# Constant products on TensorE at the heads of stages, and two pieces of VectorE work queued behind others

## The chip, the cores and the metric

The kernel runs on one core of a Trainium2 chip. The metric is the device time of one execution in microseconds; of several executions the median counts. All activations and weights are float32 in HBM.

## The reference, cut to what matters

Two models follow one another on a sequence of 256 positions with 1024 channels. The first has four layers, each an FFN, a mixer and another FFN; the mixers are sliding-window attention (layers 0 and 3), gated linear attention (1) and the recurrent mixer rwkv7 (2). The second has two layers, each a mixer (latent attention, then neighbourhood attention) and a gated FFN with a short convolution.

```python
for layer in range(4):
    ff = swiglu(rmsnorm(h, g[0]), ffn_w_in[layer, 0], ffn_w_out[layer, 0]); h = h + 0.5 * rmsnorm(ff, g[1])
    u = rmsnorm(h, g[2]);  m = (swa_attention, gla_attention, rwkv7_time_mix)[layer % 3](u, ...)
    h = h + rmsnorm(m, g[3])
    ff = swiglu(rmsnorm(h, g[4]), ffn_w_in[layer, 1], ffn_w_out[layer, 1]); h = h + 0.5 * rmsnorm(ff, g[5])
...
def step(state, inp):                 # rwkv7, one position; 16 heads of 64
    r_t, w_t, k_t, v_t, a_t, b_t = inp
    sa = jnp.einsum('bhij,bhj->bhi', state, a_t)
    state = state * w_t[:, :, None, :] + sa[..., None] * b_t[:, :, None, :] + v_t[..., None] * k_t[:, :, None, :]
    return state, jnp.einsum('bhij,bhj->bhi', state, r_t)
...
h_lat = layer_norm(DEEPNORM_ALPHA * h_lat + g1 * y, ln1_g[i], ln1_b[i])          # y from mla_mixer / na_mixer
h_lat = layer_norm(DEEPNORM_ALPHA * h_lat + g2 * conv_ffn(modulate(h_lat, sh2, sc2), ...), ln2_g[i], ln2_b[i])
```

## The kernel before

The 256 positions are two tiles of 128 partitions (`t`). Every large product is made of three fp32r products (`mm3`, L116 to L118): each operand is split into a rounded part (`whi`, `xTh`, by a copy on ScalarE, L81) and the rest (`wlo`, `xTl`, by a subtraction on VectorE, L82). `wchunk` loads a weight chunk of 128x1024 into one of four staging buffers (`st`) and splits it; `wblock` and `wmat` call it. With `held` at 0 the two split instructions are queued behind the two instructions in `split` on their engines (`issue_after`), with `held` above 0 that many chunks go before that. PSUM has three rings: `psG` (tag `G`, 2 buffers) for projections and scores, `psT` (tag `pt`, 2) for transposes and `psO` (tag `po`, 4) for accumulators. A scheduler puts the instructions of each engine in a fixed order before the run, by program order and by when it expects each to be ready; an engine then works its own list strictly in that order. `issue_after` adds an edge for the order of one engine only.

- `ffn1_body`: eleven blocks `j`, both tiles in each; first products into `G` from the transposed input `xT`.
- `swa_body`: after the projections, for each tile and for blocks of four or two heads (512 columns) scores `S`, masked softmax, transposes `pT`, product with `v`.
- `gla_body`: `proj(b)` yields a product `G` for each tile; block 1 (keys) is the first.
- `rwkv_body`: channels in two halves `q`. At its start the normalised input is transposed (`un`, `pt`, L771 to L774), then come projections, and `part1(0)`, `part2(0)`, `part1(1)`, `merges(0)`, `part2(1)`, `part3(0)`, `merges(1)`, `part3(1)`. `part1(q)` makes decays, normalised keys and the matrices `ar`, `bk`, `L` for each tile and stores `L` to DRAM. `part2(q)` reads the 16x16 diagonal blocks back (`comp`), inverts them in 15 steps of a product and a reduction on VectorE (L950, L951), copies the transpose (L952), stores both and reloads the full matrices `T` and `Z`. `merges(q)` builds the inverse of the 128x128 blocks from them (L964). `part3(q)` runs the chain R (`psR`, L1030), U (`psU`, L1036), Y (`psY`, L1055, L1057), the state, and the output norm; the gate product `psg` (L1096, L1097) stands at its end.
- `Block2.mod_T`: transposes `h` and scales it; called at the head of both mixers (`mod_tile`) and after each output tile (`conv_in`).
- `Block2.na` and `na_attn`: for each tile and each of 16 heads a score product `S` (L1598), a bias on VectorE (L1600), `softmax`, and `pv` (transposes `pP`, L1301; copy `PT`, L1303; products with `v`). The splits of `w_o` for the output product come after it in the program.

## Time and profile before

| | |
|---|---|
| median of 3 executions | 3358.42 us (3358.12 to 3369.33) |
| profiled execution, its own time | 3367.27 us |
| its span | 3365.5 us, 45238 instructions |
| TensorE products busy | 3190.7 us (95%), 16491 |
| VectorE, ScalarE, GpSimd busy | 2340.0 us (70%), 1596.2 us (47%), 161.6 us (5%) |
| mean granted clock of TensorE | 0.969 |
| HBM traffic | 156 GB/s over the span |

The profile is of one execution. Busy time of TensorE includes the time in which a product is under way, so it is not TensorE at its peak. PE is TensorE, PEld its weight loads, DVE is VectorE, ACT is ScalarE, POOL is GpSimd, SP the queue of most DMAs. The granted clock is 1.00 at 2.4 GHz and 0.50 at 1.2 GHz. L12 is line 12 of the kernel. An idle time stands in square brackets, with what ended it.

### The profile page before, as it was taken

What the parts mean: (1) busy time and instruction counts of PE and PEld (TensorE: products, weight loads), DVE (VectorE), ACT (ScalarE), POOL (GpSimd) and SP (SyncE); (2) the same over time, 40 slices, a digit from 0 to 9 for tenths busy, and PEclk for the clock granted to TensorE, in tenths of its full rate; (3) what the DMA queues carried; (4) which work ended last, traced back from release to release, by engine and by line L of the source; (5) the groups of instructions that cost most, each with busy time, mean ns of one, the idle gap of its engine ahead of it and who ended that gap; (6) DMA issues with size and microseconds to landing.
All of it is one profiled execution on the core that took longest, in us unless ns stands there. A gap on an engine that the chain in (4) does not pass through costs nothing. (4 is left out here: it accounts for less than half of the span.)

```text
span 3365.5 us, 45238 instructions
## 1 busy us (share of the span) xinstructions
PE 3190.7 (95%) x16491; PEld 2620.0 (78%) x16491; DVE 2340.0 (70%) x3767; ACT 1596.2 (47%) x2734; POOL 161.6 (5%) x248
## 2 busy tenths in 40 slices
PE   8999999989999988899999999999999999998898
PEld 7877877877887766687878877887777887775797
DVE  6767767677767766656776676765579877637787
ACT  5455454455445465224454464545544434424453
POOL 0001000000000001001010001010000000011000
PEclk9999999999999999779999999999999999998899
DMA  7653657643766753414656645631027554431463
GB/s 241 214 200 97 219 181 227 217 138 107 231 207 194 231 166 92 117 41 138 219 181 221 198 135 188 219 116 52 15 69 226 170 161 138 143 105 42 150 183 100
DMA packets 424667, 529.12 MB, mean 157 GB/s; under 512 B 54982, under 2 KB 342792, under 8 KB 424444
## 3 DMA queue, kind: packets, MB, share of 16 engines
q1 hardware_dynamic: 416124, 523.86, 49.7%
q10 hardware_dynamic: 8320, 2.36, 0.3%
q8 instruction: 130, 2.13, 0.3%
q14 instruction: 93, 0.76, 0.1%
HBM read 520.35 MB, written 5.78 MB: 156 GB/s over the span
## 5 line engine op out<-in xcount | busy, mean ns | idle before, releaser
L82 DVE TENSOR_TENSOR wlo<-st,whi 128x1024 fp32r<-128x1024 f32 (+1 forms) x810 | 974.8, 1216 | 406.4 <-ACT whi L81 371.6
L81 ACT CAST whi<-st 128x1024 fp32r<-128x1024 f32 (+1 forms) x810 | 835.5, 1044 | 532.3 <-PE po L118 171.3
L118 PE MATMUL G<-whi,xTl 128*128 128x512 f32 x1792 | 708.5, 396 | 19.8 <-DVE xTl L183 19.1
L116 PE MATMUL G<-whi,xTh 128*128 128x512 f32 x1792 | 714.1, 399 | 8.5 <-ACT xTh L802 1.9
L117 PE MATMUL G<-wlo,xTh 128*128 128x512 f32 x1792 | 705.3, 394 | 3.8 <-DVE wlo L79 3.8
L118 PEld LDWEIGHTS G<-whi,xTl 128*128 128x128 f32 x1792 | 338.5, 189 | 97.4 <-DVE xTl L183 27.1
L116 PEld LDWEIGHTS G<-whi,xTh 128*128 128x128 f32 x1792 | 338.8, 189 | 78.4 <-ACT xTh L802 3.1
L117 PEld LDWEIGHTS G<-wlo,xTh 128*128 128x128 f32 x1792 | 339.0, 189 | 71.9 <-DVE wlo L79 5.7
L116 PE MATMUL po<-whi,hh 128*128 128x512 f32 x968 | 379.6, 392 | 9.1 <-ACT hh L260 7.2
L117 PE MATMUL po<-wlo,hh 128*128 128x512 f32 x968 | 377.6, 390 | 0.0
L118 PE MATMUL po<-whi,hl 128*128 128x512 f32 x968 | 339.9, 392 | 1.0 <-DVE hl L1750 0.5
L1714 PE MATMUL G<-xh,whi 128*128 128x256 f32 (+1 forms) x720 | 244.2, 340 | 9.1 <-ACT ub L1718 5.7
L1715 PE MATMUL G<-xl,whi 128*128 128x256 f32 (+1 forms) x720 | 242.2, 336 | 0.8 <-DVE xl L1239 0.8
L1716 PE MATMUL G<-xh,wlo 128*128 128x256 f32 (+1 forms) x720 | 241.7, 336 | 0.0
L251 ACT ACTIVATE sg<-G,rpre 128x256 f32<-128x256 f32 x176 | 83.8, 476 | 290.3 <-PE G L118 285.9
L116 PEld LDWEIGHTS po<-whi,hh 128*128 128x128 f32 x968 | 181.8, 188 | 50.6 <-ACT hh L260 10.9
L118 PEld LDWEIGHTS po<-whi,hl 128*128 128x128 f32 x968 | 180.5, 188 | 40.2 <-DVE hl L261 2.0
L117 PEld LDWEIGHTS po<-wlo,hh 128*128 128x128 f32 x968 | 181.8, 188 | 37.1
L1182 DVE SCALAR_TENSOR_TENSOR aa<-aw,sc,aa 128x1024 f32<-128x1024 f32 x140 | 174.9, 1282 | 46.8 <-DMA aw<-in_ada_w_dram 46.3
L1714 PEld LDWEIGHTS G<-xh,whi 128*128 128x128 f32 x720 | 139.1, 193 | 23.6 <-ACT ub L1718 6.1
L1715 PEld LDWEIGHTS G<-xl,whi 128*128 128x128 f32 x720 | 139.2, 193 | 15.2 <-DVE xl L1239 1.3
L1716 PEld LDWEIGHTS G<-xh,wlo 128*128 128x128 f32 x720 | 138.9, 193 | 14.3
(483 smaller groups left out, 4350.1 us busy)
## 6 DMA issues: line engine op xcount, KB each, us to landing
st<-in_ffn_w_in_dram SPq DMA_DIRECT2D x704, 256.0 KB, 4.2
st<-in_ffn_w_out_dram SPq DMA_DIRECT2D x242, 512.0 KB, 4.1
aw<-in_ada_w_dram SPq DMA_DIRECT2D x96, 512.0 KB, 4.5
st<-in_ffn_w_in_dram SPq DMA_DIRECT2D x88, 512.0 KB, 5.0
st<-in_swa_w_qkv_dram SPq DMA_DIRECT2D x24, 512.0 KB, 4.8
st<-in_gla_w_in_dram SPq DMA_DIRECT2D x24, 512.0 KB, 4.5
st<-in_rwkv_w_rkv_dram SPq DMA_DIRECT2D x24, 512.0 KB, 4.6
st<-in_na_w_qkv_dram SPq DMA_DIRECT2D x24, 512.0 KB, 4.2
```

What stands on the lines that cost most here:

```text
L81: nc.scalar.copy(hi, st)
L82: nc.vector.tensor_sub(lo, st, hi)
L116: m(out, xh, wh, start=start, stop=False)
L117: m(out, xh, wl, start=False, stop=False)
L118: return m(out, xl, wh, start=False, stop=stop)
L251: nc.scalar.activation(sg, G[:, :256], AF.Tanh, scale=rs[t][1])
L1182: nc.vector.scalar_tensor_tensor(acc[s], st, x, acc[s], op0=OP.mult, op1=OP.add)
L1714: m(Gf[:, a:b], wh, xh[:, k, a:b], start=(k == 0 and a == 0), stop=False, **kw)
L1715: m(Gf[:, a:b], wh, xl[:, k, a:b], start=False, stop=False, **kw)
L1716: m(Gf[:, a:b], wl, xh[:, k, a:b], start=False, stop=(k == 7 and b == ns * 256), **kw)
```

## The change

A tile of ones, 128x1 in bf16, is made once, and a method `warm(ps, n)` issues `n` products of it (both operands by broadcast, so 128x128 against 128 x columns) into the PSUM tile that the next real product overwrites with `start=True`. It is called in ten functions. `psg` in `part3` moves up ahead of Y. In `part1(1)` everything of the second tile is traced under `issue_after(zc[0])`, so its VectorE instructions are queued behind the last copy of `part2(0)`. In `na` the splits of `w_o` are queued behind the copy `PT` and the bias of the fourth head of the first tile. The pad of the small pool shrinks by 32 bytes. Lines that only gain an indentation are left out here.

```diff
+        self.one_ = self.consts.tile([128, 1], BF16, name="one_")
+        nc.vector.memset(self.one_, 1.0)
+    def warm(self, ps, n):
+        o = ps if len(ps.shape) == 2 else ps.rearrange("p a b -> p (a b)")
+        k = o.shape[1]
+        for _ in range(n):
+            self.nc.tensor.matmul(o, self.one_.to_broadcast([128, o.shape[0]]), self.one_.to_broadcast([128, k]),
+                                  start=True, stop=True, skip_group_check=True)
...
# ffn1_body
                 G = self.psG.tile([128, 512], F32, name="G", tag="G")
+                if (j, t) == (0, 0):
+                    self.warm(G, 3)
# swa_body
             S = c.psG.tile([128, nh, nk], F32, name="S", tag="G")
+            if (nb == 1 and h0) or (t and h0 < 8):
+                c.warm(S, 3)
# gla_body, proj
+            if b == 1 and t == 0:
+                c.warm(G, 8)
# rwkv_body, front, for each t and q
             pt = c.psT.tile([128, 4, 128], F32, name="pt", tag="pt")
+            c.warm(pt, 6)
# part1
         for t in TT:
+            with c.tc.issue_after(zc[0].ins) if q and t else nullcontext():
...
                     pb = c.psT.tile([128, 2, 129], F32, name="pb", tag="pt")
+                    if q and a == 0:
+                        c.warm(pb, 5)
...
                     pt = c.psT.tile([128, 4, 128], F32, name="pt", tag="pt")
+                    if q:
+                        c.warm(pt, 2)
...
                     ps = c.psO.tile([128, 4, 128], F32, name="psL", tag="po")
+                    if q:
+                        c.warm(ps, 2)
# part2
-        nc.vector.tensor_copy(Zc, Tc.rearrange("p a b -> p b a"))
+        zc[q] = nc.vector.tensor_copy(Zc, Tc.rearrange("p a b -> p b a"))
# merges
-        def four(a, lhs, rhs, pool, tag):
+        def four(a, lhs, rhs, pool, tag, n=0):
             ps = pool.tile([128, 4, 128], F32, name="ps4", tag=tag)
+            c.warm(ps, n)
...
-                    ps = four(a, lambda hh: L[t, q][:, hh], lambda hh: Z[t, q][:, hh], c.psO, "po")
+                    ps = four(a, lambda hh: L[t, q][:, hh], lambda hh: Z[t, q][:, hh], c.psO, "po",
+                              16 if (q, t, a, B) == (0, 0, 0, LEV[0]) else 0)
# part3
             pu = c.psO.tile([128, 8, 64], F32, name="psU", tag="po")
+            c.warm(pu, 2)
...
             nc.scalar.copy(U, pu)
+            pg = c.psG.tile([128, 512], F32, name="psg", tag="G")
+            c.warm(pg, 2)
...
                 nc.tensor.matmul(py[:, hh], MB[hh % 2][:, hh // 2], hv(U)[:, hh], start=False, stop=(hh == 7),
                                  skip_group_check=True)
+                if hh % 2 and hh < 7:
+                    c.warm(pg, 1)
+            nc.tensor.matmul(pg, gmT[:, 0, t * 128:t * 128 + 128], g2a, start=True, stop=False)
+            nc.tensor.matmul(pg, gmT[:32, 1, t * 128:t * 128 + 128], g2b[:32], start=False, stop=True)
...
-            pg = c.psG.tile([128, 512], F32, name="psg", tag="G")
-            nc.tensor.matmul(pg, gmT[:, 0, t * 128:t * 128 + 128], g2a, start=True, stop=False)
-            nc.tensor.matmul(pg, gmT[:32, 1, t * 128:t * 128 + 128], g2b[:32], start=False, stop=True)
# Block2.mod_T
             pt = c.psT.tile([128, 4, 128], F32, name="pt", tag="pt")
+            if t < 2:
+                c.warm(pt, 4)
# Block2.pv(..., warm=0)
         pt = c.psT.tile([128, 4, 128], F32, name="pP", tag="pt")
+        c.warm(pt, warm)
...
-        nc.scalar.copy(PT, pt)
+        self.turned = nc.scalar.copy(PT, pt)
# Block2.na
+            c.split, c.held = self.begun, 0
             wo = c.wblock(w_o, 0, 8, 0, D)
+            c.held = -1
# Block2.na_attn
                     S = c.psG.tile([128, 512], F32, name="S", tag="G")
+                    if t == 0 and hh < 4:
+                        c.warm(S, 3)
...
-                            [[v[x][:, hh // 2, 64 * (hh % 2):64 * (hh % 2) + 64] for x in (2, 3, 0, 1)]], rev)
+                            [[v[x][:, hh // 2, 64 * (hh % 2):64 * (hh % 2) + 64] for x in (2, 3, 0, 1)]], rev,
+                            4 if t == 0 and hh < 3 else 0)
+                    if (t, hh) == (0, 3):
+                        self.begun = self.turned, biased
```

## Rows read from the trace of the kernel before

**Rows 1.** Span, first to last instruction, and mean granted TensorE clock.
```profile
core 0: 3365.5 us, clock 0.969
```
**Rows 2.** Stretches: length; busy PE, PEld, DVE, ACT, POOL; PEclk, DMA share, GB/s.
```profile
246.00:282.00 36.00, 31.20 (x232) 24.59 (x231) 31.00 (x92) 24.69 (x92) 0.00 (x0) 0.91 0.17 56
...
1340.00:1386.00 46.00, 30.55 (x116) 21.92 (x116) 31.42 (x77) 6.39 (x15) 3.81 (x4) 0.51 0.35 89
...
1426.00:1462.00 36.00, 34.32 (x157) 28.61 (x157) 14.56 (x31) 7.50 (x12) 1.93 (x2) 0.51 0.20 54
1503.00:1525.00 22.00, 20.21 (x168) 16.69 (x167) 13.69 (x31) 3.85 (x8) 1.90 (x2) 1.00 0.08 25
...
3018.00:3044.00 26.00, 16.70 (x64) 8.69 (x64) 18.75 (x35) 11.05 (x21) 2.75 (x1) 0.74 0.36 113
...
3139.00:3172.00 33.00, 20.49 (x122) 18.46 (x121) 28.69 (x51) 15.91 (x26) 2.82 (x4) 0.74 0.60 190
```
**Rows 3.** Timeline of TensorE, single products: start, length, engine, line, operation [idle before].
```profile
698.97 0.63 PE L116 MATMUL G<-whi,xTh 128*128 128x512 f32 x1
699.39 0.63 PE L117 MATMUL G<-wlo,xTh 128*128 128x512 f32 x1
...
1007.87 0.19 PE L1203 MATMUL psa<-one,ab 128*128 128x1 bf16 x2
...
1329.96 0.39 PE L118 MATMUL G<-whi,xTl 128*128 128x512 f32 x1
1330.18 0.39 PE L116 MATMUL G<-whi,xTh 128*128 128x512 f32 x1
...
1499.55 1.08 PE L1096 MATMUL psg<-g2a,gmT 128*128 128x512 f32 x2
```
**Rows 4.** Waits of TensorE: total us, times, longest us.
```profile
PE G L118 <- DVE xTl L183: 19.1, 14, 3.4
...
PE pt L773 <- ACT un L771: 9.9, 2, 7.3
```
**Rows 5.** Timeline of VectorE, first and last of eleven operations, and the copy.
```profile
1363.19 0.42 DVE L875 TENSOR_SCALAR th<-th 128x512 f32<-128x512 f32 x1
...
1371.96 0.68 DVE L926 TENSOR_TENSOR bk<-pt,E 128x512 f32<-128x512 f32 x1
...
1373.55 0.38 DVE L952 COPY Zc<-Tc 128x256 f32<-128x256 f32 x1
```
**Rows 6.** Timeline of TensorE, first merge products of each half.
```profile
1386.45 6.43 PE L964 MATMUL ps<-Z,L 128*128 128x128 f32 x30 [12.24 <-DMA Z<-Zd]
...
1471.52 1.95 PE L964 MATMUL ps<-Z,L 128*128 128x128 f32 x16
```
**Rows 7.** Timeline of TensorE, the four psU of part3.
```profile
1426.91 3.67 PE L1036 MATMUL psU<-W,Z 128*128 128x64 f32 x16 [1.27 <-ACT W L1033]
...
1457.62 3.68 PE L1036 MATMUL psU<-W,Z 128*128 128x64 f32 x16
...
1503.47 2.00 PE L1036 MATMUL psU<-W,Z 128*128 128x64 f32 x16
...
1522.18 2.00 PE L1036 MATMUL psU<-W,Z 128*128 128x64 f32 x16
```
**Rows 8.** Timeline of TensorE, transposes in mod_T.
```profile
2252.11 1.03 PE L1229 MATMUL pt<-ident,h 128*128 128x128 f32 x8
```
**Rows 9.** Timeline of VectorE, ScalarE and TensorE at the neighbourhood attention.
```profile
3026.56 1.23 DVE L82 TENSOR_TENSOR wlo<-st,whi 128x1024 fp32r<-128x1024 f32 x1
...
3028.20 1.04 ACT L81 CAST whi<-st 128x1024 fp32r<-128x1024 f32 x1 [1.68 <-DMA st<-in_na_w_o_dram]
...
3029.97 2.07 PE L1598 MATMUL S<-kT,qT 64*128 64x512 f32 x2 [8.25 <-ACT P L1284]
...
3044.11 1.46 PE L1598 MATMUL S<-kT,qT 64*128 64x512 f32 x4
...
3048.39 1.45 PE L1598 MATMUL S<-kT,qT 64*128 64x512 f32 x4
```

More of the change, by code (lines that the diff above doesn't have):

```diff
@@ L1 @@
 import math
-from contextlib import ExitStack
+from contextlib import ExitStack, nullcontext
 import numpy as np
@@ L886, in part1 @@
-            Es[t] = E1, E2
-            e = mix.tile([128, 4], F32, name=f"em{t}{q}")
-            nc.vector.tensor_copy(e, E2[:, :, 0] if t else E1[:, :, 128])
-            E1m[t, q] = e
-            z = c.psO.tile([128, 512], F32, name="z", tag="po")
-            nc.tensor.matmul(z, waT[1][:, t * 128:t * 128 + 128], wa2[1][:65], start=True, stop=True)
-            th_a[t] = tmp("tha")
-            nc.scalar.activation(th_a[t], z, AF.Tanh, scale=0.5)
-            km = tmp("km", 1)
-            nc.vector.scalar_tensor_tensor(km, th_a[t], -1.0, kab, op0=OP.add, op1=OP.mult)
@@ L907, in part1 @@
-            b2 = th_a[t]
-            nc.vector.scalar_tensor_tensor(b2, b2, 1.0, kn, op0=OP.add, op1=OP.mult)
-            bo = tmp("bo")
-            nc.vector.tensor_mul(bo, r[t, q], km)
-            nc.vector.tensor_mul(bo, bo, rkb)
-            bon[t, q] = mix.tile([128, 8], F32, name=f"bon{t}{q}")
-            nc.vector.tensor_reduce(bon[t, q], hv(bo), axis=AX.X, op=OP.add)
-            if not q:
-                ar[t, q], bk[t, q] = ring([128, 4, 2, 128], "ar"), ring([128, 4, 2, 128], "bk")
-            else:
-                ar[t, q] = c.act.tile([128, 4, 2, 128], F32, name="ar", tag="xTh")
-                bk[t, q] = c.act.tile([128, 4, 2, 128], F32, name="bk", tag="xTl")
@@ L920, in part1 @@
-            E1, E2 = Es[t]
-            for x, dst, e in ((kn, ar[t, q][:, :, 0], E1[:, :, :128]), (r[t, q], ar[t, q][:, :, 1], E1[:, :, 1:]),
-                              (b2, bk[t, q][:, :, 0], E2[:, :, 1:]), (km, bk[t, q][:, :, 1], E2[:, :, 1:])):
-                pt = c.psT.tile([128, 4, 128], F32, name="pt", tag="pt")
-                for ch in range(4):
-                    nc.tensor.transpose(pt[:, ch], x[:, ch * 128:(ch + 1) * 128], c.ident)
-                nc.vector.tensor_mul(dst, pt, e)
@@ L927, in part1 @@
-            L[t, q] = ring([128, 8, 128], "L")
-            for a in range(2):
-                ps = c.psO.tile([128, 4, 128], F32, name="psL", tag="po")
-                for i in range(4):
-                    p = slice(64 * a, 64 * a + 64)
-                    nc.tensor.matmul(ps[:, i], ar[t, q][p, i, 0], bk[t, q][p, i, 0], start=(i == 0),
-                                     stop=(i == 3), skip_group_check=True)
-                nc.vector.tensor_mul(L[t, q][:, 4 * a:4 * a + 4], ps, mL.unsqueeze(1).to_broadcast([128, 4, 128]))
@@ L939, in part2 @@
+    T, Z, zc = {}, {}, {}
     def part2(q):
@@ L1294, in more, with pv @@
         return self.c.work.tile(shape, F32, name=name, tag=tag)
-    def pv(self, M, out, P, vs, order=None):
+    def pv(self, M, out, P, vs, order=None, warm=0):
         c, nc = self.c, self.c.nc
         pt = c.psT.tile([128, 4, 128], F32, name="pP", tag="pt")
+        c.warm(pt, warm)
         for j in range(4):
```

92 lines of the change are left out of this document (64 added, 28 removed).

## The prediction

> **What bounds the kernel now.** I read the clock first, then a table of stretches, then the instructions of the few stretches that stand out. The mean granted clock is 0.969 over a span of 3365.5 us [rows 1]. Only two levels are granted, 2.4 GHz (1.00) and 1.2 GHz (0.50), so about 3365.5 × 0.031 / 0.5 = 209 us ran at half speed. The slices show where: long dense stretches (the FFNs) stand at 1.00, and the low digits sit at the heads of stages and in the recurrent mixer. The table of stretches gives them a cause [rows 2]. In 1426 to 1462 us the clock is 0.51 and TensorE is busy 34.32 of 36 us: there a slow TensorE *is* the time. In 1340 to 1386 us it is 0.51 too, but TensorE has 15 us of idle time and VectorE works 31.42 of 46 us: there the slow clock lies partly beside other work. At the start of the neighbourhood attention (3018 to 3044 us) TensorE is busy 16.70 of 26 us at 0.74, at its end (3139 to 3172 us) 20.49 of 33 us at 0.74, while VectorE is busy 28.69. So a better clock is worth much in one stretch and little in most others; elsewhere the kernel is bound by TensorE at full speed, and there each added product costs its own length.
>
> **What is added.** From the diff I count 254 products of 512 columns (FFN heads 8×3, sliding-window scores 2×7×3, gla 8, rwkv front 24, part1 24, merges 16, part3 4×7, mod_T 64, neighbourhood heads 24) and 10 of 258 columns. No row shows a bf16 product of 512 columns. The nearest below is a bf16 product of one column (two in 0.19 us), the nearest above one pass of an fp32 product of 512 columns (two in 1.08 us, some 0.5 each); between them lies the fp32r product of 512 columns, which starts every 0.22 us at full clock and every 0.42 us at half [rows 3]. I take 0.23 us (0.43 at half clock), because the columns are the same and each is one record; all 254 are then 58 us. The ends, 0.05 and 0.5 us, are kept for the range. What counts is how many stand in a wait.
>
> **Heads of FFN, gla and rwkv.** The first products there wait already: 19.1 us in 14 waits for the low half of the activations, the longest 3.4 us, and 9.9 us in two waits (one of 7.3 us) for the normalised rows of rwkv [rows 4]. Three products are 0.7 us, so at the FFN heads I charge 1 us in all (5.5 if nothing hides them, 0 if all do). In gla eight products (1.8 us) stand in such a wait; the products at 698.97 us, 0.42 us apart, show that the clock had fallen [rows 3], and about ten of them return 0.2 us each: −2 (0 to −2). The 24 at the rwkv front (5.5 us) fit into the 9.9 us of waits; VectorE and ScalarE set the pace there, so −1 (−2 to +2).
>
> **Sliding-window attention, twice.** 36 us at 0.91 [rows 2] are 6.5 us of half clock, in which TensorE is busy for some 4 us; a full clock returns 2. The 21 products (4.8 us) write into the ring of two score buffers, so they start only when the real scores could, and TensorE has 4.8 us of idle time in all. I charge half: +0.3 per layer, +0.6 together (−4 to +6).
>
> **The recurrent mixer, VectorE order.** The 16-step inverse of the first half (L950 to L952) ends with the copy at 1373.55 us. Between 1363.19 and 1371.96 us eleven operations of the second half's second tile stand among its steps: the 0.42 us one and ten of 128x512, each 0.6 us of pitch (0.68 long) [rows 5], 6.3 us, and up to three more earlier (kn, its square sum, its scaling). The new order puts them behind the copy: the inverse ends 6.3 to 8.1 us sooner, I take 7.5. With it go the two stores and four loads of T and Z on SP, which follow the inverse, and the first merge product, which now waits 12.24 us for the last of them [rows 6]. What is moved has to fit into that wait: 6.3 us of VectorE work and two tiles of L do; its store of L on ScalarE's queue and the reload of `comp` come about when they come now, since they are behind the same `L`. If they come later, the second inverse is late instead: up to +4 is kept for the range.
>
> **Merges.** Sixteen products (6.9 us at half clock) stand in the 12.24 us wait. The first 30 real ones take 6.43 us; at full clock 16 take 1.95 us, so 30 take 3.7 [rows 6]: −2.8 (0 if the clock doesn't rise). In part1 of the second half 34 products (6.5 us) go into 46 − 30.55 = 15 us of idle time [rows 2]; the gain of a better clock and what doesn't fit are put at 0 (−2 to +5).
>
> **part3.** The same chain runs twice. In the first half, from the first psU to the end of the second, it takes 1426.91 to 1461.30 = 34.4 us at half clock; in the second half 1503.47 to 1524.18 = 20.7 us at full clock [rows 7], with more work of others in between. If the products (7 per tile, in the waits for R and U and between the psY products) hold the clock, 13.7 us come back, less 2.5 of the 3.2 us that they take: −11.2. In the second half, at full clock already, they only cost: +2.5. The gate product psg, moved ahead, is issued early in the first tile already and is put at 0.
>
> **mod_T.** Sixteen products in each of four places. Three of them are dense: the transposes of `h` at 2252 us, for example, stand in a run of products [rows 8], and there is no wait to fill. 48 × 0.23 = 11 us; I take 7, as some land in nearby waits. At the end of the neighbourhood mixer TensorE has 12.5 us of idle time and a clock of 0.74 [rows 2], 17 us of half clock, in which it is busy for some 8; VectorE covers part of that. I put 3 as the gain and 1.5 of the 16 products' 3.7 us as the cost: −1.5 (−3 to +2).
>
> **Neighbourhood attention.** Five splits of `w_o` (1.23 us each on VectorE) are issued among the first softmaxes, and the exponentials of the first heads stand on ScalarE behind a cast that waits for its load until 3028.20 us; the third score product waits 8.25 us for them [rows 9]. Once the heads run, two take 4.28 us (3044.11 to 3048.39). Without the splits heads 3 to 6 would follow from 3021 us at that pace, so the scores at 3044.11 us would stand at about 3034.5: −9.6. Back come eight splits behind the fourth head, 1.23 us each, 9.8 us, of which I charge 3 since VectorE has slack between heads, and 24 products, 5.5 us, of which 1.6 is not in a wait: −5 (−9 to +5). Their loads stay longer in the four staging buffers and hold up the FFN's first weights behind them on SP, which are needed only after the attention.
>
> **Sum.** 1 − 2 − 1 + 0.6 − 7.5 − 2.8 + 0 − 11.2 + 2.5 + 7 − 1.5 − 5 = −19.9 us. The profiled execution took 3367.27 us, so it would take 3347.4; it is 8.85 us above the median of 3358.42, and the same difference from the median gives 3338.5 us.
>
> **The rivals.** (a) *The clock doesn't hold in part3.* TensorE is busy for 34.32 of 36 us there and the clock stays down all the same [rows 2], so more work alone need not raise it. Then 13.7 is lost and 14 products cost 0.2 more: 3338.5 + 13.7 + 2.8 = 3355. Against it: in the second half nearly the same work runs at 1.00. (b) *The constant products displace real ones, and the kernel gets slower.* The gains above sum to 2 + 1 + 4 + 7.5 + 2.8 + 13.7 + 3 + 6.6 = 41 us (4 for the two sliding windows, 3 and 6.6 for the neighbourhood mixer's end and start). 41 / 0.23 = 178: from 178 products on the path on, the kernel is slower. With all 254 on it the time is 3358.4 + 58 − 41 = 3375. For it: the dense places, where there is nothing to fill; against it: 24 + 16 + 8 products stand before waits that are longer than they are [rows 4, 6]. The Trainium skill (TensorE: Matmul & The Clock Gate, Part 2, step 1) says that products stay in program order and only weight loads are pulled ahead, by which every constant product ahead of a ready one is paid in full; no row here has such a product. (c) *More than the sum:* the dense places take nothing, and in 1340 to 1386 us half of TensorE's 30.55 us comes back as well: 3358.4 − 41 − 15 = 3302. (d) *All cold time is paid back.* 209 us at half speed returning half of itself would be 104 us, 3254; VectorE's share in 1340 to 1386 us and TensorE's idle time in the other half-clock stretches speak against it [rows 2]. The Trainium skill (TensorE: Matmul & The Clock Gate, Terms) prices throttled time in this way, time × (1 − K/N).
>
> **How the numbers follow.** The sum as it stands has 0.58, with 3318 to 3352 as its own range; (a) 0.20, (b) 0.12, (c) 0.07, (d) 0.03. The price of a product moves about 80 on the path by −14 to +22 us. A range from 3308 to 3364 leaves out (d), most of (c) and the slower half of (b). About 0.5% (16.8 us) is what a measurement can tell from no change: faster means below 3341.6. Of the sum's 0.58 some 0.48 lie there, with (c) and (d) 0.58; above 3375 lies some 0.07 of (b) and the price.
>
> **What would show it.** Granted clock 1.00 in the part3 stretch, which shrinks from 34 to about 23 us; the inverse of the first half ending some 7 us sooner against the last `proj`; the first merge at full clock; the third score product of the neighbourhood attention some 8 us sooner; three mod_T places each 2 to 4 us longer. I am wrong if part3 stays at 0.5, or if the dense FFN stretches grow.

## The result, and the profile after

The change made the kernel slower: 3405.93 us (median of 4, 3395.20 to 3410.23) against 3360.59 us for the kernel before, a ratio of 1.0123 (95% interval 1.0102 to 1.0144), some 41 us by the ratio (45 between the medians). The forecast was 3338.5 us. The profiled execution took 3408.12 us, 40.9 us more than that of before.

First the clock, and the table of stretches of the changed kernel, as in [rows 1, 2] (length; busy time and count of TensorE, its loads, VectorE, ScalarE, GpSimd; granted clock; DMA share; GB/s):

```profile
core 0: 3406.3 us, clock 0.972
```

```profile
246.00:282.00 36.00, 34.40 (x252) 25.09 (x251) 30.98 (x92) 24.38 (x91) 0.00 (x0) 1.00 0.18 56
1340.00:1386.00 46.00, 36.86 (x178) 24.54 (x179) 31.26 (x76) 6.61 (x17) 4.58 (x4) 0.74 0.37 92
1423.00:1456.00 33.00, 27.12 (x172) 22.78 (x170) 15.04 (x31) 8.63 (x12) 1.93 (x2) 0.77 0.25 91
1502.00:1542.00 40.00, 39.33 (x206) 31.31 (x205) 15.01 (x32) 4.66 (x9) 1.91 (x2) 0.70 0.05 14
...
3062.00:3094.00 32.00, 27.10 (x113) 16.16 (x112) 23.86 (x45) 17.61 (x31) 4.51 (x1) 0.73 0.59 164
3047.00:3160.00 113.00, 105.54 (x469) 60.47 (x467) 71.15 (x167) 49.16 (x103) 11.17 (x3) 0.88 0.21 56
```

The clock did what the change is named for: 0.91 became 1.00 in the sliding-window attention, 0.51 became 0.74 at 1340 us and 0.77 in part3's first half. The half-clock time fell from 209 to 3406.3 × 0.028 / 0.5 = 191 us. And the kernel is slower.

To see where, each VectorE instruction of the kernel before was matched with the same one after (same line of the program, same tile, same occurrence), and the median shift of its end taken over stretches of 20 us. A column names the start of its stretch in the time of before; minus is earlier. The eight kernels that are as before up to 1200 us (b_order, c1, c2, c2b, c3, c5, c5b, c5r) stand 1.5 to 9 us later there, so a shift of a few us is within what two profiles differ by.

| us of before | 300 | 1200 | 1330 | 1400 | 1465 | 1560 | 2200 | 2300 | 2480 | 2900 | 3020 | 3120 | 3350 |
|---|---|---|---|---|---|---|---|---|---|---|---|---|---|
| after, shift in us | 0.4 | -0.2 | 0.5 | -4.1 | -4.0 | 18.3 | 21.1 | 24.2 | 29.9 | 30.8 | 22.8 | 42.1 | 40.8 |
| only the VectorE order (b_order) | 1.1 | 2.0 | 3.9 | -3.0 | -2.5 | -0.6 | -1.2 | -2.7 | -2.7 | -5.0 | -6.0 | -5.8 | -6.4 |
| without part3's products (a_no_p3) | 0.8 | 3.7 | 2.4 | -1.2 | 1.0 | 4.6 | 4.9 | 6.5 | 10.5 | 12.3 | 5.4 | 15.8 | 14.4 |
| without mod_T's products (a_no_modT) | 1.9 | 4.2 | 2.1 | -2.5 | -0.5 | 20.1 | 23.1 | 23.9 | 26.1 | 23.4 | 16.2 | 29.4 | 29.1 |
| c2 (no products, see below) | 3.0 | 2.7 | 2.9 | -4.3 | -16.3 | -12.7 | -10.7 | -12.0 | -10.6 | -11.7 | -19.6 | -24.0 | -27.2 |

Three places make the loss: part3's second half (1465 to 1560, +22.3), mod_T (2200 to 2900, +9.7) and the neighbourhood heads (3020 to 3120, +19.3, after a gain of 8 at their start).

TensorE's waits in the changed kernel (total us, times, longest):

```profile
PE pt L186 <- DVE yc L1129: 7.6, 1, 7.6
PE pb L903 <- DVE th L894: 5.0, 2, 4.4
PE psY L1087 <- ACT U L1067: 4.9, 2, 4.3
...
PE ps L990 <- DMA Z<-Zd: 2.9, 1, 2.9
```

The 12.24 us before the first merge [rows 6] are 2.9 now. In their place stand new waits: for the norm of part3's last tile (`yc`, 7.6), for `th` of part1's moved tile, and for `U`. The wait for `U` is in part3's first half. ScalarE there:

```profile
1424.19 1.04 ACT L92 CAST whi<-st 128x1024 fp32r<-128x1024 f32 x1 [5.44 <-DMA st<-in_rwkv_w_o_dram]
1425.45 1.04 ACT L92 CAST whi<-st 128x1024 fp32r<-128x1024 f32 x1 [0.22 <-DMA st<-in_rwkv_w_o_dram]
...
1426.89 2.09 ACT L92 CAST whi<-st 128x1024 fp32r<-128x1024 f32 x2
1428.88 0.58 ACT L1067 COPY U<-psU 128x512 f32<-128x512 f32 x1
```

psU ends at 1425.2 us, 5.3 us sooner than before. Its copy is last in a row behind four casts of the output weights, which wait for their loads. TensorE stands 4.27 us, and the clock falls in that wait: psY behind it runs at 0.43 us a product.

In the kernel before, the same casts held up another copy, that of `R` (the trace calls it `W`, the name of the buffers it is put in):

```profile
1425.33 1.04 ACT L81 CAST whi<-st 128x1024 fp32r<-128x1024 f32 x1 [0.95 <-DMA st<-in_rwkv_w_o_dram]
1426.28 0.58 ACT L1033 COPY W<-psR 128x512 f32<-128x512 f32 x1
...
1430.62 0.59 ACT L1039 COPY U<-psU 128x512 f32<-128x512 f32 x1 [1.39 <-PE psU L1036]
```

There TensorE stood 1.27 us for `R` ahead of psU [rows 7]. The clock fell in that wait, at 1426.6 us, and stayed at half for 37.6 us. The copy of `U` waited only for psU itself, and TensorE for `U` only 0.25 us. In the changed kernel `R` is copied ahead of the casts (1418.16 us), and the wait has moved from `R` to `U` and grown.

In the second half, TensorE and VectorE:

```profile
1502.32 2.00 PE L1064 MATMUL psU<-W,Z 128*128 128x64 f32 x16
...
1527.67 2.16 PE L65 MATMUL psg<-one__73 128*128 128x512 bf16 x5
...
1538.37 0.83 PE L65 MATMUL G<-one__73 128*128 128x512 bf16 x3
1539.03 1.89 PE L1064 MATMUL psU<-W,Z 128*128 128x64 f32 x16
```

```profile
1521.08 0.69 DVE L1129 TENSOR_TENSOR yc<-yc,psg 128x512 f32<-128x512 f32 x1
1521.68 0.75 DVE L1048 TENSOR_TENSOR MK<-psK,mK 128x256 f32<-128x256 f32 x2
...
1526.98 0.76 DVE L1048 TENSOR_TENSOR MK<-psK,mK 128x256 f32<-128x256 f32 x2 [0.69 <-PE psK L1044]
```

The two psU are 36.7 us apart; before it was 18.7 [rows 7]. Between them TensorE's list now holds 22 products of w_o (`po`) and the three constant products of the *next* FFN, none of which stood there before; and VectorE makes the last two pairs of `MK` of the second tile behind the end of the first tile's norm. Before, both pairs came ahead of it:

```profile
1516.25 0.75 DVE L1021 TENSOR_TENSOR MK<-psK,mK 128x256 f32<-128x256 f32 x2
...
1518.71 0.75 DVE L1021 TENSOR_TENSOR MK<-psK,mK 128x256 f32<-128x256 f32 x2
...
1521.06 0.69 DVE L1098 TENSOR_TENSOR yc<-yc,psg 128x512 f32<-128x512 f32 x1
```

No line of the diff asks for this. The scheduler orders each engine's list by when it expects an instruction to be ready; with more products in the list it expects other times, and orders everything anew.

### The profile page after: what moved, and what is told of

The parts are those of the page before. It is cut to its first block, busy times and chain, and to the rows that moved or that the text cites. A ratio compares the mean times of both kernels' runs of the same rounds, so it can differ in the third digit from the quotient of the medians.

```text
span 3406.3 us, 45743 instructions
## 1 busy us (share of the span) xinstructions
PE 3266.7 (96%) x16755; PEld 2649.9 (78%) x16755; DVE 2337.6 (69%) x3768; ACT 1597.0 (47%) x2734; POOL 162.2 (5%) x248
## 4 chain that ended last, share of the span: by engine, by line
PE 69%; issue 18%; DVE 6%; ACT 4%; DMA 2%; POOL 1%; SPq 0%; ACTq 0%; POOLq 0%; DVEq 0%
PE G L129 8%; PE G L127 8%; PE G L128 8%; PE po L127 6%; PE po L128 6%; PE po L129 6%; PE G L1756 3%; PE G L1757 3%; PE G L1758 3%; PE po L1341 2%; PE ps L990 1%; DVE wlo L93 1%; PE pP L1335 1%; PE S L1494 1%; PE S L1637 1%
## 5 line engine op out<-in xcount | busy, mean ns | idle before, releaser
L93 DVE TENSOR_TENSOR wlo<-st,whi 128x1024 fp32r<-128x1024 f32 (+1 forms) x802 | 962.4, 1212 | 379.2 <-ACT whi L92 336.4
L92 ACT CAST whi<-st 128x1024 fp32r<-128x1024 f32 (+1 forms) x802 | 827.2, 1044 | 502.7 <-PE po L129 156.5
L129 PEld LDWEIGHTS G<-whi,xTl 128*128 128x128 f32 x1792 | 339.7, 190 | 96.2 <-DVE xTl L194 27.1
L1756 PEld LDWEIGHTS G<-xh,whi 128*128 128x128 f32 x720 | 138.6, 193 | 20.1 <-ACT ub L1760 3.0
```

What stands on the lines that cost most here:

```text
L92: nc.scalar.copy(hi, st)
L93: nc.vector.tensor_sub(lo, st, hi)
L129: return m(out, xl, wh, start=False, stop=stop)
L1756: m(Gf[:, a:b], wh, xh[:, k, a:b], start=(k == 0 and a == 0), stop=False, **kw)
```

## The experiments

Ratios are to the kernel before, timed on the same chip in the same rounds, with the 95% interval. The first four kernels each undo one part of the change or make one alone.

**One part undone: part3's constant products (a_no_p3).**

```diff
-            c.warm(pu, 2)
-            c.warm(pg, 2)
-                if hh % 2 and hh < 7:
-                    c.warm(pg, 1)
```

> The changed kernel without the 28 constant products of part3 (the gate product stays ahead). Theory (the constant products of part3 take places ahead of ready ones and move the half-clock stretch from the first half into the second): the second half's part3 is back at clock 1.00, about 34 us from first scores of its chain to its end instead of 57, and the time falls by 15 to 20 us to about 3388. Rival (the clock falls in either half because the copy of U waits behind four casts of the output weights, with or without constant products): one of the two halves stays at 0.5 to 0.75 and the time stays within 6 us of 3406.

Measured: 1.0048 (1.0033 to 1.0063), 3385.76 us; some 25 us less than with them. The step at 1465 to 1560 us falls from 22.3 to 3.6, the two psU of the second half are 20.3 us apart, and no product of `po` stands between them. The time is as the theory has it. In the first half nothing is lost by taking the products out: 33 us from psU to psU against 30 to 36 us in the kernels with them and with the casts where they were. There the rival's cause is seen: TensorE waits 3.77 us for `U`, and the clock is at half for 37.6 us, without a constant product. So 28 products of 0.22 us, 6 us in all, cost some 20, nearly all of it in the second half.

**One part undone: mod_T (a_no_modT).**

```diff
-            if t < 2:
-                c.warm(pt, 4)
```

> The changed kernel without the 64 constant products of mod_T. Theory (three of the four places are dense and pay each product, as forecast at +7, with -1.5 at the fourth): the steps of +3 us at 2260, +4 at 2480 and +3 at 2850 us between the two traces go, and the time falls by 6 to 10 us to about 3398. Rival (these steps are clock that fell anew in the dense stretches of the second model): they stay, and the time is within 3 us of 3406.

Measured: 1.0058 (1.0041 to 1.0075), 3391.07 us. From 2200 to 2900 us the shift rises by 0.3 instead of 9.7: the part is worth 9.4 us in this pair of profiles, as the theory has it (the same shift rises by 5.4 to 8.6 us in the five other kernels with these products). The time fell by more than the theory had, 22 us by the ratios. Some 6 us of the rest lie at 3020 to 3120 us (13.2 instead of 19.3), where the clock stood better in this run; what is left can't be placed, as the profiled execution (3396.47 us) was 5 us above the median. How dense the places are is seen in the changed kernel:

```profile
2277.29 1.04 PE L65 MATMUL pt<-one__73 128*128 128x512 bf16 x4
2278.17 0.60 PE L1262 MATMUL pt<-ident,h 128*128 128x128 f32 x4
```

Four products push the transposes back by 0.88 us, 0.22 each: 48 of them are 10.6 us, nearly all of it paid. The Trainium skill (TensorE: Matmul & The Clock Gate, Part 2, step 1) has products in program order; these rows agree, 0.22 us for each constant product ahead of a transpose.

**One part alone: the VectorE order (b_order).** The kernel before, with nothing but

```diff
+            with c.tc.issue_after(zc[0].ins) if q and t else nullcontext():
```

> The kernel before with only the new order of VectorE: the second tile of part1's second half queued behind the last copy of the first inverse; no constant product. Theory (the inverse ends 6.2 us sooner, and the second inverse waits for its blocks about as long as before, so the gain is small): the first merge starts some 6 us sooner, the first psU of part3 0 to 4 us sooner, the time within 4 us of 3360. Rival (as forecast, the order alone brings 7.5 us): 3353.

Measured: 0.9975 (0.9963 to 0.9986), 3360.90 us against 3369.03 on that chip. The shift goes from 3.9 at 1330 us to -3.0 at 1400: 6.9 us (4.7 to 7.9 in the seven other kernels with this order and no constant products there). Of these, 4.5 are left at 1560 us. The rival, which was the forecast's own step (7.5 us), was right: the ratio is worth 8.4 us. The first merge of this kernel runs at full clock without any constant product:

```profile
1384.33 3.62 PE L977 MATMUL ps<-Z,L 128*128 128x128 f32 x30
```

Thirty products take 3.62 us; before they took 6.43 [rows 6]. The moved tile's own transposes and `psL` now fill the wait.

**Order or length in part3: the old order put back around all 28 products (a_p3ord).** The products of w_o are queued behind psU of the second tile, the end of the first tile's norm behind the second tile's `MK`:

```diff
+        with c.tc.issue_after(pui[0].ins):        # last product of psU
+            po = c.out_proj(oT, wo)
...
+            if t:
+                with c.tc.issue_after(mki.ins):   # last MK of this tile
+                    late.pop()()                  # bonus and gate of the first tile
```

> The changed kernel with all 28 constant products of part3, and the order of the kernel before put back around them in part3's second half: the products of w_o are queued behind psU of the second tile on TensorE, and the end of the first tile's norm (bonus and gate) behind the second tile's MK on VectorE. Theory (part3's second half loses its 20 us because the added products made the scheduler put 38 products of w_o ahead of psU, so that the norm of the second tile comes late and TensorE stands 7.6 us before its transpose; not through the products' own length and not through the clock): that wait falls below 2 us, psU of the second tile follows that of the first by 19 to 25 us instead of 30 to 37, and the time falls by 10 to 17 us to about 3393. Rival (the clock or the products' own length is the loss): the stretch stays within 5 us and the time within 5 us of 3406.

Measured: 1.0104 (1.0088 to 1.0119), 3399.22 us. The wait of 7.62 us before the transpose of `yc` is gone, the psU are 25.6 us apart (36.7 without the order), and the step at 1465 to 1560 us is 10.5 instead of 22.3. The whole time fell by less than expected, 6 us by the ratios: in the profiled run 4.7 us were lost before part3 is reached (shift 5.2 at 1330 us, 0.5 in the changed kernel), where the two kernels do the same. So half of the 20 us is the order. Of the 10.5 that are left, 3.6 are there in a_no_p3 too, and 6.9 stand between the psU (25.6 against 18.7), where the clock falls:

```profile
1509.00:1538.00 29.00, 27.56 (x175) 23.25 (x174) 13.72 (x31) 4.37 (x9) 1.90 (x2) 0.76 0.07 19
```

29 us at 0.76 are 14 us of half clock; half of that is 7 us. The length of the seven products between the psU, 1.5 us, is in the 6.9 too.

**The wait for U taken away (a_wo2).** As a_p3ord, and the output weights' casts and splits queued behind the copy of `U` and the last `MB` of part3's first tile:

```diff
+    c.split, c.held = begun[0], 0
     wo = c.wblock(w_o, 0, 8, 0, D)
+    c.held = -1
```

> As the run with part3's order put back, and besides the casts and splits of the output weights are queued behind the copy of U and the last MB of part3's first tile. Theory (in the first half the clock falls because TensorE stands 4.27 us before the product with U, whose copy waits on ScalarE behind four casts of output weights that come when their loads land, and the constant products stand before that wait, not in it): the wait falls below 1.5 us, part3's first half runs at 1.00 for most of its length, its two psU are 20 to 25 us apart instead of 30, and the time is 5 to 12 us below the run with the order alone. Rival (the clock falls there whatever stands in the wait): the clock stays at 0.75 or below between the two psU and the time within 3 us of the run with the order alone.

Measured: 1.0034 (1.0013 to 1.0056), 3380.61 us, 18.6 us below a_p3ord. The first half's stretch, ScalarE and TensorE in it:

```profile
1425.00:1451.00 26.00, 24.73 (x175) 20.69 (x176) 14.81 (x32) 8.54 (x12) 1.93 (x2) 0.87 0.36 124
```

```profile
1427.98 0.58 ACT L1073 COPY U<-psU 128x512 f32<-128x512 f32 x1 [2.39 <-PE psU L1070]
1428.47 3.88 ACT L89 CAST whi<-st 128x1024 fp32r<-128x1024 f32 x4
```

```profile
1425.95 2.00 PE L1070 MATMUL psU<-W,Z 128*128 128x64 f32 x16
...
1448.91 2.00 PE L1070 MATMUL psU<-W,Z 128*128 128x64 f32 x16
```

The psU of the first half are 23.0 us apart (36.3 in a_p3ord, 30.7 before), and the wait for `U` is 0.67 us (3.51 in a_p3ord). That is the theory's case, with more time than it had: by the shifts 13 us come between 1400 and 1465 us, and 3 more in the neighbourhood heads. Nothing was added to TensorE for it; four casts of 1 us moved behind a copy.

**Are the constant products needed there at all (c2, c3)?** c2 is the kernel before with b_order's order, the casts of w_o moved as above, and the spread of the neighbourhood's `w_o` (c1, below), so it differs from c1 by the move of the casts alone. It holds no constant product. c3 adds 14 of them in part3's first half.

> The kernel before with the VectorE order in the recurrent mixer, w_o of the neighbourhood attention spread over the pairs of heads, and the casts of the recurrent mixer's output weights behind the copy of U; no constant product anywhere. Theory (in part3's first half the wait for U is the cause of the fall of the clock, but without constant products the clock is already at 0.50 when part3 begins, since the merges come at the end of a stretch at 0.5, so taking the wait away alone gains little): the two psU of the first half stay 28 to 31 us apart and the time is within 4 us of 3347. Rival (the wait alone holds the clock down): they come to 21 to 25 us and the time falls to about 3338.

> As c2, with 14 constant products in part3's first half only, and the gate product ahead. Theory (constant products hold the clock where no wait follows them, and where the list keeps its order they cost little): the two psU of the first half are 21 to 25 us apart at clock 0.9 or more, part3's second half stays at 1.00 with psU 18 to 20 us apart, and the time is 6 to 10 us below c2, about 3338. Rival (the products only hold the clock together with those of part1 and merges ahead of them): 28 us or more, time as c2.

Measured: c2 0.9929 (0.9903 to 0.9956), 3341.04 us; c3 0.9955 (0.9936 to 0.9974), 3351.28 us. The theory fell, in both runs: without any constant product the clock comes back by itself. In c1, as in the kernel before, TensorE waits for `R` and not for `U`:

```profile
1422.26 3.68 PE L1053 MATMUL psU<-W,Z 128*128 128x64 f32 x16 [1.21 <-ACT W L1050]
```

In c2 that wait is gone. Its first half, as stretch, on ScalarE and on TensorE:

```profile
1421.00:1447.00 26.00, 25.23 (x161) 21.78 (x160) 15.38 (x32) 7.95 (x11) 1.93 (x2) 0.74 0.27 80
```

```profile
1423.92 0.59 ACT L1056 COPY U<-psU 128x512 f32<-128x512 f32 x1 [4.81 <-PE psU L1053]
1424.40 3.89 ACT L92 CAST whi<-st 128x1024 fp32r<-128x1024 f32 x4
```

```profile
1421.27 2.61 PE L1053 MATMUL psU<-W,Z 128*128 128x64 f32 x16
...
1424.56 0.69 PE L1075 MATMUL psY<-U,MB 128*128 128x64 f32 x2 [0.25 <-ACT U L1056]
...
1444.42 2.00 PE L1053 MATMUL psU<-W,Z 128*128 128x64 f32 x16
```

The clock falls all the same, 1.2 us after psU has begun (psY at 0.43 us a product), but it is back after 13.7 us; in c1 it falls at the same place and is at half for 37.5 us. The next psU of c2 takes 2.00 us: they are 23.2 us apart, where c1 has 30.7 and c3 24.5. c2's shift from 1400 to 1465 us is -12.0 (c1: -0.1); the forecast had -11.2 for this step, from the constant products. Over all profiles the psU of the first half are 29.7 to 36.3 us apart in the nine with the casts where they were, and 19.9 to 29.3 in the eight with the casts moved, six of them with constant products (20.9 to 29.3) and two without (19.9 and 23.2). That moving the casts brings it is shown; why the clock then comes back sooner, though it falls as before, is not.

**All products that stand in waits (c4).** c3 with those of part1, the merges, the sliding windows, gla, the rwkv front and the FFN heads as well.

> As c3, with the constant products of part1, the merges, the sliding-window attention, gla, the front of the recurrent mixer and the FFN heads as well; without those of mod_T, of part3's second half and of the neighbourhood heads. Theory (these places wait already, so their products cost nothing and gain little: the clock of the stretches rises, but VectorE and the loads set their end): the time is within 5 us of c3, and the half-clock time falls by 50 us or more without a like gain. Rival (a quicker clock there is worth half its time, some 15 to 25 us): the time is 12 us or more below c3.

Measured: 0.9956 (0.9939 to 0.9973), 3351.18 us, as c3. The half-clock time by the clocks below is 3338.4 × 0.025 / 0.5 = 167 us in c2, 167 in c3 and 120 in c4 (c2, c3, c4 in this order):

```profile
core 0: 3338.4 us, clock 0.975
```

```profile
core 0: 3344.8 us, clock 0.975
```

```profile
core 0: 3345.6 us, clock 0.982
```

47 us less at half clock, and no time gained. In the profiles c4 is 3.2 us ahead of c3 by 2900 us and loses 4.1 in the neighbourhood heads, for which both have the same list (below), so a gain of some 3 us may be hidden; the rival's 12 are not. That VectorE and the loads set the end in these places is argued; at 1340 to 1386 us the clock is 0.79 in c4 and VectorE is busy 33.1 of 46 us (31.4 at clock 0.51 before [rows 2]). The Trainium skill (TensorE: Matmul & The Clock Gate, Terms) would price these 47 us at 23.5; the run shows none of it.

**The second half again (c5, c5b, c5r).** c3 with the second half's 14 products too, order kept; c5b is c5 once more; in c5r the products read 16 different columns and a weight that differs from row to row instead of ones.

> As c3, with the 14 constant products of part3's second half too, and the order of the kernel before kept around them. Theory (what is left of the second half's loss, 8 to 10 us with the order put back, is the products' own length at a clock that they don't keep up): psU of the second half's two tiles are 23 us or more apart instead of 18.7, the clock falls below 0.9 between them, and the time is 5 to 9 us above c3. Rival (with the order kept the products cost only their length, 14 times 0.23 = 3.2 us, less what falls into waits): 2 us above c3 or less.

> c5 once more, for a second profile. Theory (the clock falls in part3's second half wherever constant products stand ahead of psU there): it falls again within the 12 us after the first psU of the second half, and the two psU of that half are 23 us or more apart. Rival (the fall in c5 was chance): the half runs at 1.00 and they are 20 to 22 us apart.

> c5 with the same list of instructions, but the added products read varied numbers instead of ones (16 different columns, and a weight that differs from row to row). Theory (what is in the operands doesn't matter, the products' place does): as c5, the clock falls in part3's second half and its two psU are 23 us or more apart. Rival (constant operands don't keep the clock up): the clock stays at 1.00 in that half, psU 20 to 22 us apart, and the time is 4 to 8 us below c5.

Measured: c5 0.9971 (0.9955 to 0.9987), 3357.17 us; c5b 0.9966 (0.9952 to 0.9979); c5r 0.9955 (0.9940 to 0.9969). The psU of the second half are 25.8, 25.5 and 25.4 us apart; in c4, with none there, 18.7. The stretch in c5, c5b and c5r:

```profile
1500.00:1529.00 29.00, 27.50 (x174) 23.25 (x174) 13.72 (x31) 4.27 (x8) 1.91 (x2) 0.76 0.06 19
```

```profile
1492.00:1521.00 29.00, 27.81 (x175) 23.38 (x175) 13.83 (x31) 4.38 (x9) 1.91 (x2) 0.76 0.06 19
```

```profile
1486.00:1514.00 28.00, 26.81 (x172) 22.57 (x171) 13.45 (x31) 3.64 (x8) 1.90 (x2) 0.76 0.06 20
```

The theory held for the distance and the clock in all three; c5r's time is 4.6 us below c5's, with intervals that overlap. So the fall isn't chance and isn't the ones. It is no private property of the products either: c2b, below, fell there without any.

**The neighbourhood heads (a_no_na, a_pair, c1).** a_no_na undoes the three edits of this part. a_pair keeps them and forces the heads into pairs: transposes of a pair behind the scores of both heads, products with `v` behind the transposes of both.

```diff
# a_pair, in na_attn, for each pair of heads
+                    with c.tc.issue_after(scored.ins):   # score of the second head
+                        ...                              # transposes of both
+                    with c.tc.issue_after(turn.ins):     # last transpose
+                        ...                              # products with v of both
```

c1 is b_order with those pairs, and with one chunk of `w_o` behind each pair of the first tile, instead of all eight behind the fourth head:

```diff
+                    if t == 0:
+                        c.marks.append((self.turned, biased))
# wchunk, held == 0
+            if self.marks:
+                self.split = self.marks.pop(0)
```

> The changed kernel with the neighbourhood attention as before: no constant products at its heads, and the splits of w_o where they were. Theory (the splits, put behind the fourth head, stand among the running heads and cost there more than their leaving the first heads brings: 5 us gained until the eighth head, 7 to 10 lost until the twelfth): the first to the last bias take about 100 us instead of 111, the wait at the third score product is back at about 8 us, and the time falls by 5 to 10 us to about 3398. Rival (the heads lost their pairs in the list through edits elsewhere, and the splits are innocent): the heads still take 105 us or more from first to last bias and the time stays within 4 us of 3406.

> The changed kernel with the heads of the neighbourhood attention kept in pairs: the transposes of a head's pair are queued behind the scores of both heads, the products with v behind the transposes of both. In the changed kernel's trace one head alone takes 2.66 us (scores at 3106.36 and 3109.02), in the trace of before two heads take 4.28 us. Theory (the order of TensorE's list lost the pairs, in which two products on different halves of the rows run side by side): 2.66 - 2.14 = 0.52 us per head come back over some 25 heads, the time falls by 10 to 13 us to about 3394, and the product S in pairs is 1.45 us for two heads. Rival (the splits of w_o that now stand among the heads, 8 of 1.23 us on VectorE, and the half clock they bring are the whole loss): the time stays within 3 us of 3406.

> The kernel before with the new VectorE order in the recurrent mixer, no constant product, the heads of the neighbourhood attention kept in pairs, and the splits of w_o spread: one chunk behind each pair of heads of the first tile. Theory (the splits cost because six of them stand within 11 us; spread over eight pairs they fit into VectorE's slack): the first to the last bias take 88 to 94 us instead of 96, the first score waits of 8 us go, and the time falls 4 to 8 us below the 3361 of the order alone, to about 3355. Rival (VectorE or ScalarE has no slack between the pairs): the heads take as long as before and the time stays at 3361 or above.

Measured: a_no_na 1.0109 (1.0074 to 1.0144), a_pair 1.0081 (1.0066 to 1.0096), c1 0.9948 (0.9933 to 0.9963). The time of a_no_na can't be told from that of the changed kernel. In its trace the heads take 102.8 us from first to last bias (after 111.4, before 96.2), between theory and rival. The stretch of the heads in a_no_p3, a_no_modT, a_no_na and a_pair (that of after is above):

```profile
3028.00:3130.00 102.00, 95.36 (x459) 55.44 (x458) 69.01 (x163) 48.06 (x100) 12.75 (x3) 0.95 0.23 63
```

```profile
3040.00:3145.00 105.00, 96.98 (x457) 56.32 (x457) 70.47 (x165) 48.18 (x100) 11.70 (x3) 0.93 0.23 61
```

```profile
3040.00:3144.00 104.00, 96.66 (x439) 55.70 (x438) 64.64 (x164) 43.30 (x97) 9.29 (x2) 0.87 0.18 46
```

```profile
3040.00:3145.00 105.00, 97.89 (x478) 59.02 (x479) 69.02 (x168) 49.29 (x104) 12.80 (x3) 0.90 0.22 61
```

And before, for the same heads:

```profile
3018.00:3118.00 100.00, 83.00 (x446) 52.49 (x446) 71.72 (x162) 44.10 (x99) 11.76 (x3) 0.88 0.19 51
```

Read together: in the list of the kernel before 20 of the 32 scores stand in pairs; in those of a_no_p3, a_no_modT and after none does, in that of a_no_na two, in that of a_pair ten. A pair of scores takes 1.46 us [rows 9], two apart take 1.12 each (at 3106.36 us in the changed kernel, say), since the heads of a pair use different halves of the rows. Without pairs TensorE is busy 93% of the stretch and sets the pace (83% before), so there the clock matters: with 10, 15 and 27 us at half clock (102 × 0.05 / 0.5, and so on) the shift from 2900 to 3120 us is +3.5, +6.0 and +11.3 us, some 0.45 us for each us at half clock (a_p3ord and a_wo2, without pairs too, have 27 and 24 us there, and +11.7 and +8.7). On that line a_pair, with 21 us, would lose 8.5; it lost 2.7. By the ratios it is 14 us faster than the changed kernel (its theory: 10 to 13). a_no_na, with 27 us, would lose 11; it lost 6.0. So with the edits of this part undone more than half of the 11.3 us is still lost: it comes with the other edits, which leave two of the 32 scores in pairs. What the pairs and the edits are worth apart, some 6 and 5 us by this line, is an estimate from single profiles; part of it may be the collisions told below, which are shorter in these two.

c1 has the same splits without such a loss. They stand 5.2 to 6.1 us apart on VectorE (the first two at 3023.84 and 3029.44 us).

In the changed kernel six of them stand between 3066.36 and 3078.75 us, in the middle of the stretch that is at 0.73. c1's heads take 87.7 us from first to last bias; from 2900 to 3120 us its shift falls by 12.2 us. Its list has 26 scores in pairs. Whether the spread or the forced pairs bring more wasn't tried apart.

Nor does the list alone set the time. c1, c2, c2b, c3, c4, c5, c5b and c5r have the same list for the heads, and take 87.4 to 96.3 us from first to last bias (b_order 95.8); from 2900 to 3120 us their shift falls by 4.0 to 12.2 us (b_order 0.8). What differs is what VectorE does while GpSimd adds `cm` to the bias table `B`, some 4.5 us, twice among the heads. Scaling a head's `P` takes VectorE 0.48 us. In c4:

```profile
3033.80 5.11 DVE L1324 TENSOR_SCALAR P<-P,sx 128x512 f32<-128x512 f32 x2
3033.94 4.69 POOL L1635 TENSOR_TENSOR B<-B,cm 128x2048 f32<-128x2048 f32 x1 [26.32 <-DVE sx L1322]
...
3039.06 1.04 PE L1653 MATMUL pP<-rev,P 128*128 128x128 f32 x4 [3.60 <-DVE P L1324]
```

The second of the two scalings starts beside the addition and takes 4.7 us, TensorE stands 3.60 us for it, and at the end of that wait the clock falls (3039.1 us). A scaling of over 4 us comes not once in c1, c2 and c2b (87.4 to 88.6 us), once in c3 and c5b (92.0 and 92.6), twice in c4, c5 and c5r (95.9 to 96.3). The kernel before and b_order have two of 3.3 to 3.9 us. So some 3 to 4 us of c1's gain are there with both collisions, and the rest is that c1 has none. No run keeps the two engines apart on purpose.

**The version that beats both, once more (c2b).**

> c2 once more, in more rounds, to settle its time against the kernel before: 0.993 of it, an interval that ends below 0.996; part3's first half again at clock 0.8 or more without any constant product, psU 21 to 25 us apart.

Measured: 0.9917 (0.9896 to 0.9938), median 3337.50 us. With c2's 0.9929 that is 24 to 28 us below the kernel before and 65 to 69 below the changed one. The profiled execution of c2b was the slowest of its six (3360.49 us; the other five took 3334 to 3338), and the clock fell in its second half, without a constant product in the kernel:

```profile
1430.00:1452.00 22.00, 20.21 (x155) 16.29 (x155) 14.69 (x32) 7.45 (x10) 1.93 (x2) 0.92 0.28 87
1492.00:1524.00 32.00, 30.55 (x164) 25.34 (x163) 13.47 (x31) 4.03 (x8) 1.90 (x2) 0.63 0.06 17
```

Its first half, which began at full clock, took 19.9 us from psU to psU, again without one.

## Why the prediction was wrong

The direction was wrong: -19.9 us was forecast, +40.9 came. Step by step, in the profiled executions:

| step | forecast | measured | from |
|---|---|---|---|
| price of a product | 0.23 us | 0.22 us | rows of mod_T |
| heads of FFN, gla, front, sliding windows | -1.4 | 0 to +0.5 | shift at 1200 us, and 20.8 to 21.3 over layer 3 |
| VectorE order | -7.5 | -6.9 | b_order, shift from 1330 to 1400 us |
| merges, part1's second half | -2.8 | +2.3 | -4.6 after, -6.9 in b_order |
| part3, first half | -11.2 | 0.1 | shift from 1400 to 1465 us |
| part3, second half | +2.5 | +22.3 | shift from 1465 to 1560 us |
| mod_T, dense | +7 | +9.4 | a_no_modT |
| end of the neighbourhood mixer | -1.5 | -1.3 | shift from 3120 to 3350 us |
| start of the neighbourhood attention | -5 | +11.3 | shift from 2900 to 3120 us |

The measured rows sum to some 38; the rest is between them.

- **The price and the dense places were right.** The products cost what the nearest rows said, and where nothing waits they are paid.
- **The VectorE order was right,** in size and mechanism. It is the one part of the change that gains. The merges' gain of 2.8 was counted twice: the order alone brings the first merges to full clock, with real work moved into the wait.
- **part3, first half: the wrong cause.** The step took "half clock" for the cause and "more products" for the cure. psU did run at full clock (2.00 us instead of 3.67) and ended 5.3 us sooner, but it does so in a_no_p3 too, without the products: in both `R` is copied ahead of the casts of the output weights. Then TensorE stood 4.27 us for `U`, whose copy now was behind the casts, and the clock fell there: 30.2 us from psU to psU after 30.7. The 13.7 us that the sum took back depended on ScalarE's list, which the prediction doesn't look at. What brought them was the casts out of the way (-12.0 us in c2, without a product). Rival (a) had this outcome and its argument, that work alone need not raise the clock, but no mechanism either. The trace of before had a hint: psU waits for `W` from ScalarE [rows 7], behind a cast. It had no wait for `U` to see (0.25 us); that one came with the new order.
- **part3, second half: a term that wasn't in the sum.** I charged the products' length, 2.5 us. Some 11 us were the order of the list, which the products changed, and some 7 a fall of the clock with the products' own length. Rival (b) had the sign and "displaced", but priced it by the products' own time, 58 us if all 254 were on the path. What displaced was not the products: it was 22 products of w_o that they made the scheduler move ahead of psU.
- **The neighbourhood heads: an order not seen, and slack not looked at closely enough.** The gain at the start came (-8). The eight splits were charged 3 us on "slack between heads"; but six of them stood in 12 us, in which three heads ran. How much of the loss they are isn't shown: with the edits undone (a_no_na) 6.0 of the 11.3 us stay. The larger part is what the sum had no term for: with the edits elsewhere the heads lose their pairs, TensorE is busy 93% of the stretch instead of 83%, and sets the pace.
- **The slices of half clock were no budget.** Rivals (c) and (d) held that more of it might come back. c4 gave back 47 us of half clock for nothing that can be told. Half clock cost time in part3 and in the unpaired heads, where TensorE is busy over 90%. Elsewhere it comes together with waits: in the eight kernels with the spread the heads take 88 us with 7 us of half clock and 96 with 17, and the collisions bring both the waits and the clock's fall.

Left open: why the clock falls in part3's second half. It did in all nine profiles with constant products there, whatever their operands, and in one of eight without (two more show some 3 us of it). Which products change which list wasn't tried one by one, nor the move of psg alone, nor whether all three edits of the neighbourhood part cost, or the splits alone.

## What to carry to other kernels

Before filling an engine's waits, find the instruction that ends each wait and move what stands ahead of it: four casts moved behind one copy gave some 12 us in part3, eight splits spread over eight forced pairs 3 to 11 in the attention (eight kernels against b_order), and neither added a product for the clock. Such an instruction can be on another engine than the one that is waited for, as the additions on GpSimd were. In a kernel whose order a scheduler works out, an added instruction can change the lists after it; compare the lists first, and put back with explicit order what was good. Time at half clock is a loss where that engine sets the pace, so price it by stretch, with the busy share and the waits beside the clock.

## What the runs showed of the hardware

- The granted clock of one kernel isn't the same from run to run: the four executions of the changed kernel took 3395 to 3410 us at mean clocks of 0.972 to 0.977, and in c2b one of six was 23 us behind the others at 0.969 (the others 0.976 to 0.978).
- The clock came back by itself in c2 within part3's first half, after 13.7 us at half speed, with no wait of TensorE over 0.52 us in it; in c1, with a wait of 1.21 us ahead of the same products, it was at half for 37.5 us. In stretches: 26 us at 0.74 are 13.5 us at half clock; before, 36 us at 0.51 were 35 [rows 2].
- Ones, or varied numbers, in the added products made no difference to the clock (25.5 and 25.4 us between the psU of c5b and c5r).
- Two products that use different halves of the rows run side by side: two scores in 1.46 us together, 1.12 each apart.
- A VectorE scaling of 128x512 that takes 0.48 us took 4.6 to 4.7 us where it began with an addition of 4.5 us on GpSimd (c3, c4, c5, c5b, c5r), and ended within 0.3 us of that addition's end.
